# Score products over all 128 rows, and weights laid out tile by tile, in a hybrid decoder layer

## The chip, the cores and the metric

The kernel runs on one core of a Trainium2 chip. The metric is device time in microseconds (us) from one launch to its end. The core has a matrix engine (TensorE, PE in the rows; its weight loads are shown apart as PEld), a vector engine (VectorE, DVE), a scalar engine (ScalarE, ACT), a general engine (GpSimd, POOL), a queue that only issues transfers (SyncE, SP), and 16 DMA engines.

## What is computed

One layer of a decoder on 1024 tokens of width 1024, in float32. The parts that the change touches:

```python
z = rms_norm(x) @ w_in                       # sgu u and v, q, k, value
q, k: 4 heads, 2 maps each, 64 wide          # differential attention
s = q @ k.T - slope * distance, causal       # per head and map
a = softmax(s[map 0]) - lam * softmax(s[map 1]);  o = a @ v
x = x + concat(sgu, o) @ w_out
x = x + memory_attention(x, mem)             # w_q_mem, w_kv_mem, w_o_mem; 256 memory tokens
x = x + moe(x)                               # top group, then top 2 of its 8 experts; 32 experts
#   expert: (silu(xb @ w_gate[e]) * (xb @ w_up[e])) @ w_down[e]
```

## The kernel before

A float32 product is built from three products of rounded parts: high by high, low by high, high by low (the helper mm3, L141 to L143). So each weight tile is loaded raw (128 partitions by 1024 numbers, 512 KB), then copied on ACT to a rounded high part whi (L286) and subtracted on DVE to a low part wlo (L287). One list, plan, holds all weight tiles in the order of use. pump issues the loads from SP (L277) a set number of tiles ahead, and take hands a split tile to the stage that uses it. SP is a queue in program order: a load that waits holds up the loads behind it. raw, whi, wlo and the larger activations share one pool of 45 slots of 512 KB (unit), so a load can also wait for a slot to come free.

The source of a tile decides its runs, the stretches of memory that are contiguous for one partition. A tile of 128 columns of w_in, w_kv_mem or w_out is read in runs of 512 B, a pair tile of 256 columns (w_in, md) and the memory tokens (memT) in runs of 1 KB, w_gate and w_up in runs of 2 KB, and w_down, w_q_memT and w_o_mem in runs of 4 KB. md and vwd are products of memory and weights that the kernel itself writes to DRAM (from POOL's queue) and reads back as weight tiles: md is written in runs of 1 KB; vwd is written in runs of 4 KB and read in runs of 512 B.

The program runs in this order: projections of the first head (0 to 35 us; x tiles come in on SP among the first weight tiles), memory keys and values with 16 tiles of w_kv_mem (35 to 92), attention with the other projections as filler between its steps (68 to 410), products of memory and weights and the output projection (403 to 580), memory attention (580 to 800), routing (to 843), the 32 experts (843 to 1430), and a final norm. A planner (Merge) fixes the order within a stage by estimated costs; the engines then follow that order.

In attention, a head has four tiles for q and k of 128 partitions by 1024 tokens, and one for k's low part. qa holds map 0's rounded q in partitions 0 to 63 and its low part in 64 to 127; qb holds map 1's the other way round. ka and kb hold the rounded k, once in each half of the partitions; the second half is a copy by a DMA on POOL's queue (L579, 64 by 512 numbers, 128 KB; four per head, for ka and kb and for each half of the tokens). kl holds k's low part, map 0 in partitions 0 to 63 and map 1 in 64 to 127. The score of a block of 128 queries is then, for each map and each piece of up to 512 keys, one product over 128 rows, q (high and low) by k's high part (L632), and one over 64 rows, q's high part by k's low part (L633). Their sum goes to DVE (L635), then ACT (L639) and POOL (L646).

The gate and up products of an expert use 8 tiles, the down product 4. From expert 16 on the loads run at most 10 tiles ahead (before that, up to 31).

Of the kernel before, what the change touches and what calls it, by code (L numbers as in the profile page):

```python
# [8 lines left out]
F32 = mybir.dt.float32  # L9
F32R = mybir.dt.float32r  # L10
# [8 lines left out]
S = 1024  # L19
D = 1024  # L20
# [94 lines left out]
def tile_layer(tc, a, out):  # L115
# [71 lines left out]

    kmd = dram.tile([128, KT, 256], F32, name="kmd")
    vmd = dram.tile([128, KT, 256], F32, name="vmd")
    md = dram.tile([D, D], F32, name="md")  # L190
    vwd = dram.tile([D, D], F32, name="vwd")
    mixd = dram.tile([896, S], F32, name="mixd")
    x1d = dram.tile([D, S], F32, name="x1d")
    x2d = dram.tile([S, D], F32, name="x2d")
# [18 lines left out]

    plan = []

    def add_cols(w, c0):
        plan.append((w[:, c0:c0 + 128], 8))

    def add_pair(w, c0):
        for q in range(2):  # L220
            plan.append((w[q * 512:(q + 1) * 512, c0:c0 + 256], 4))

    w_in = a["w_in"]
    for item in (SEQ1 + " " + SEQ2).split():
        kind, i = item[0], int(item[1:])
        if kind == "s":
            add_pair(w_in, 512 + 256 * i)
            add_cols(w_in, 256 * i)
            add_cols(w_in, 256 * i + 128)
        elif kind == "k":  # L230
            for c in range(4 * i, 4 * i + 4):
                add_cols(a["w_kv_mem"], c * 128)
        elif kind in "qx":
            add_cols(w_in, 1024 + 128 * i)
            add_cols(w_in, 1536 + 128 * i)
        elif kind == "v":
            add_pair(w_in, 2048 + 256 * i)
        elif kind == "f":
            add_cols(a["w_out"], i * 128)
        else:  # L240
            w = a["w_q_memT" if kind == "m" else "w_o_mem"]
            for k in (2 * i, 2 * i + 1):
                plan.append((w[k * 128:(k + 1) * 128, :], 1))
    for hd in range(4):
        add_pair(md, hd * 256)
    for h in range(2):
        for f in range(8):
            add_cols(vwd, f * 128)
    wg, wu, wd = a["w_gate"], a["w_up"], a["w_down"]

    work = [("g", 0)]
# [5 lines left out]
    for kind, e in work:  # L257
        if kind == "g":
            for w in (wg, wu):
                for q in range(4):  # L260
                    plan.append((w[e, q * 256:(q + 1) * 256, :], 2))
        else:
            for k in range(4):
                plan.append((wd[e, k * 128:(k + 1) * 128, :], 1))
# [5 lines left out]
    def pump():  # L270
        while ptr["load"] < min(len(plan), ptr["use"] + ahead["load"]):
            j = ptr["load"]
            src, k = plan[j]
            raw = unit("raw", [128, 1024])
            r3_, s3 = raw.rearrange("p (k c) -> p k c", k=k), src.rearrange("(k p) c -> p k c", p=128)
            for i in ((0, 4), (4, 8)) if j == 0 else ((0, k),):
                nc.sync.dma_start(r3_[:, i[0]:i[1]], s3[:, i[0]:i[1]])  # L277
            raws[j] = raw
            ptr["load"] += 1
        while ptr["split"] < min(ptr["load"], ptr["use"] + ahead["split"]):  # L280
            j = ptr["split"]
            raw = raws.pop(j)
            hi = unit("whi", [128, 1024], F32R)
            lo = unit("wlo", [128, 1024], F32R)
            for c in (slice(0, 512), slice(512, 1024)) if j == 0 else (slice(0, 1024),):
                nc.scalar.copy(hi[:, c], raw[:, c])  # L286
                ahead.get("lo", nc.vector).tensor_tensor(lo[:, c], raw[:, c], hi[:, c].bitcast(F32), op=OP.subtract)  # L287
            parts[j] = (hi, lo)
            ptr["split"] += 1
# [11 lines left out]

    def load_mem(q):
        m = unit("memt", [128, 4, 256])
        nc.sync.dma_start(m, a["memT"][q * 512:(q + 1) * 512, :].rearrange("(k p) t -> p k t", p=128))
        memt.append(m)

    def split_mem(q):
# [83 lines left out]
    def mem_m(hd):  # L391

        kk = kks.pop(("m", hd))
        w = [take() for _ in range(2)]
        for g in range(2):
            mt = unit("mt", [128, 4, 256])
            for b in range(2):
                p = ps1("pp")
                for j in range(2):
                    ds_ = slice((4 * g + 2 * b + j) * 128, (4 * g + 2 * b + j + 1) * 128)  # L400
                    for d in range(2):
                        mm3(p[:, j * 256:(j + 1) * 256], w[d][0][:, 0, ds_], w[d][1][:, 0, ds_], kk[:, 0, d],
                            kk[:, 1, d], d == 0, d == 1)
                nc.scalar.copy(mt[:, 2 * b:2 * b + 2], p)
                yield 1.3, 0.0
            nc.gpsimd.dma_start(md[g * 512:(g + 1) * 512, hd * 256:(hd + 1) * 256].rearrange(
                "(k p) c -> p k c", p=128), mt)

    def mem_w(hd):

        vk = kks.pop(("w", hd))
        w = [take() for _ in range(2)]
        for b in range(2):
            bs_ = slice(b * 128, (b + 1) * 128)
            mt = unit("mt", [128, D])
            for c in range(2):
                cs = slice(c * 512, (c + 1) * 512)
                p = ps1("pp")
                for d in range(2):
                    mm3(p, vk[:, 0, d, bs_], vk[:, 1, d, bs_], w[d][0][:, 0, cs], w[d][1][:, 0, cs], d == 0, d == 1)  # L420
                nc.scalar.activation(mt[:, cs], p, AF.Copy, scale=mcol[:, b:b + 1])
                yield 1.3, 0.0
            nc.gpsimd.dma_start(vwd[hd * 256 + b * 128:hd * 256 + (b + 1) * 128, :], mt)


    hTh = [None] * KT
# [126 lines left out]

    def evacs(hd):

        r0, r1 = slice(0, 64), slice(64, 128)

        def evac_q(h, p):
            hs = slice(h * H, (h + 1) * H)
            if h == 0:  # L560
                qk[hd] += [unit(n, [128, S], F32R) for n in ("qa", "qb")]
            qa, qb = qk[hd]
            q = scaled(h, p)
            sc = 0.125 / slopes[hd]
            for t, r, o in ((qa, r0, r1), (qb, r1, r0)):
                nc.scalar.activation(t[r, hs], q[r], AF.Copy, scale=sc)
                nc.vector.scalar_tensor_tensor(t[o, hs], q[r], sc, t[r, hs].bitcast(F32), op0=OP.mult,
                                               op1=OP.subtract)

        def evac_k(h, p):  # L570
            hs = slice(h * H, (h + 1) * H)
            if h == 0:
                qk[hd] += [unit(n, [128, S], F32R) for n in ("ka", "kb", "kl")]
            ka, kb, kl = qk[hd][2:]
            k = scaled(h, p)
            for t, r, o in ((ka, r0, r1), (kb, r1, r0)):
                nc.scalar.copy(t[r, hs], k[r])
                nc.vector.tensor_sub(kl[r, hs], k[r], t[r, hs].bitcast(F32))
                KQ(nc).dma_start(t[o, hs], t[r, hs])  # L579

        return evac_q, evac_k

# [26 lines left out]
    def scores():  # L609
# [5 lines left out]
        for hd in range(4):  # L615
            for x in until(("qk", hd)):
                yield x
            qa, qb, ka, kb, kl = qk.pop(hd)
            for i in range(8):
                if 8 * hd + i - 2 * ndone[0] >= NA:  # L620
                    yield 0.0, lambda: 8 * hd + i - 2 * ndone[0] < NA
# [2 lines left out]
                stt = sm.tile([128, 8], F32, name="stt", bufs=4)  # L624
                pr = []
                for m in range(2):
                    r = slice(m * 64, m * 64 + 64)
                    q, k = (qa, ka) if m == 0 else (qb, kb)
                    s = ps2("ps_s")
                    for c0 in range(0, nk, 512):  # L630
                        c1 = min(nk, c0 + 512)
                        mm(s[:, c0:c1], q[:, q0:q0 + 128], k[:, c0:c1], start=True, stop=False)  # L632
                        mm(s[:, c0:c1], q[r, q0:q0 + 128], kl[r, c0:c1], start=False, stop=True)  # L633
                    pe = half("p%d" % m) if i < HP else unit("p%d" % m, [128, S])
                    nc.vector.tensor_tensor_reduce(out=pe[:, :nk], in0=s[:, :nk], in1=bias[:, 896 - q0:1024],  # L635
                                                   scale=1.0, scalar=NEG, op0=OP.add, op1=OP.max,
# [837 lines left out]
    with tc.If(nr > 0):  # L1474
# [59 lines left out]
        with tc.For_i(0, nr, 1) as b:  # L1534
# [16 lines left out]
            for w in (wg, wu):  # L1551
                p = ps1()
                for q in range(4):
                    raw = unit("oraw", [128, 2, 512])
                    nc.sync.dma_start(raw, w[bass.ds(eb, 1), q * 256:(q + 1) * 256, :].rearrange(
                        "a (k p) c -> p (a k) c", p=128))
                    for k2 in range(2):
                        k = 2 * q + k2
                        mm(p, xt[:, k * 128:(k + 1) * 128], raw[:, k2], start=(k == 0), stop=(k == KT - 1))
# [62 lines left out]
def _arrays(inp):  # L1622
# [2 lines left out]
    f = {n: np.asarray(v) for n, v in inp.items()}  # L1625
    r = {}
    r["xT"] = c(f["x"][0].T)
    r["memT"] = c(f["mem"][0].T)
    for n in ("norm_mix", "norm_xq", "norm_mem", "norm_ffn"):
        r[n] = c(f[n][0].reshape(8, 128).T)  # L1630
    r["norm_ffn_row"] = c(f["norm_ffn"])
# [6 lines left out]
    for n in ("lambda_q1", "lambda_k1", "lambda_q2", "lambda_k2", "b_router_group", "b_router_expert"):  # L1638
        r[n] = c(f[n])
    r["w_q_memT"] = c(f["w_q_mem"][0].T)  # L1640
    for n in ("w_in", "w_out", "w_kv_mem", "w_o_mem", "w_router_group", "w_router_expert", "w_gate",
              "w_up", "w_down"):
        r[n] = c(f[n][0])
    return {"in_" + n: v for n, v in r.items()}


# [18 lines left out]
```

## Time and profile before

| | before |
|---|---|
| median of 3 runs | 1466.63 us (1462.87 to 1467.89) |
| the profiled execution | 1463.22 us, its span 1461.5 us |
| busy in the span: PE, DVE, ACT, POOL | 1365.2, 1008.1, 834.6, 255.4 us |
| packets moved by DMA | 188088, 320.28 MB; 86179 of them under 2 KB |

The profile follows one execution. Busy time counts an engine's own instructions; a matrix product's start is exact, while its end is modelled, so the pace of products is read from one start to the next. "Idle before" of an instruction is the time its engine waited, with what released it. PEclk is the granted clock of TensorE as a share of full speed.

### The profile page before, as it was taken

What the parts mean: (1) busy time and instruction counts of PE and PEld (TensorE: products, weight loads), DVE (VectorE), ACT (ScalarE), POOL (GpSimd) and SP (SyncE); (2) the same over time, 40 slices, a digit from 0 to 9 for tenths busy, and PEclk for the clock granted to TensorE, in tenths of its full rate; (3) what the DMA queues carried; (4) which work ended last, traced back from release to release, by engine and by line L of the source; (5) the groups of instructions that cost most, each with busy time, mean ns of one, the idle gap of its engine ahead of it and who ended that gap; (6) DMA issues with size and microseconds to landing.
All of it is one profiled execution on the core that took longest, in us unless ns stands there. A gap on an engine that the chain in (4) does not pass through costs nothing. (4 is left out here: it accounts for less than half of the span.)

```text
span 1461.5 us, 20484 instructions
## 1 busy us (share of the span) xinstructions
PE 1365.2 (93%) x7420; PEld 1153.7 (79%) x7420; DVE 1008.1 (69%) x1593; ACT 834.6 (57%) x1136; POOL 255.4 (17%) x273
## 2 busy tenths in 40 slices
PE   7989999999999999999999589999989999999981
PEld 5887878878878888999888468888778888877860
DVE  6745666656667544333454779999979999988875
ACT  7533444334445544332322368888868888777863
POOL 3131110211002222112112211111111111111012
PEclk9989999999999999999999699999999999999995
DMA  9540101102046676113699599999999899999984
GB/s 295 160 112 1 44 30 59 58 29 66 30 150 205 225 239 206 35 37 99 179 306 348 193 314 322 361 330 350 344 365 347 303 366 345 354 359 359 362 283 196
DMA packets 188088, 320.28 MB, mean 219 GB/s; under 512 B 15491, under 2 KB 86179, under 8 KB 187984
## 3 DMA queue, kind: packets, MB, share of 16 engines
q1 hardware_dynamic: 163040, 272.14, 53.5%
q0 software_dynamic: 16496, 38.41, 9.1%
q10 hardware_dynamic: 8448, 8.39, 1.7%
q8 instruction: 59, 0.97, 0.3%
q14 instruction: 45, 0.37, 0.1%
HBM read 287.10 MB, written 46.66 MB: 228 GB/s over the span
## 5 line engine op out<-in xcount | busy, mean ns | idle before, releaser
L287 DVE TENSOR_TENSOR wlo<-raw,whi 128x1024 fp32r<-128x1024 f32 (+1 forms) x467 | 554.7, 1226 | 99.2 <-ACT whi L286 82.6
L286 ACT CAST whi<-raw 128x1024 fp32r<-128x1024 f32 (+1 forms) x469 | 473.9, 1049 | 85.0 <-DMA raw<-in_w_down 21.9
L141 PE MATMUL pgu<-whi,xth 128*128 128x512 f32 x512 | 199.2, 398 | 7.6 <-ACT whi L286 7.6
L142 PE MATMUL pgu<-wlo,xth 128*128 128x512 f32 x512 | 201.7, 394 | 1.4 <-DVE wlo L287 1.4
L143 PE MATMUL pgu<-whi,xtl 128*128 128x512 f32 x512 | 201.4, 393 | 0.3 <-DVE xtl L147 0.3
L1415 POOL DMA_INDIRECT x2d<-y,idx x31 | 50.9, 1643 | 471.1 <-ACT y L1414 413.4
L141 PEld LDWEIGHTS pgu<-whi,xth 128*128 128x128 f32 x512 | 97.3, 190 | 29.5 <-ACT whi L286 10.0
L142 PEld LDWEIGHTS pgu<-wlo,xth 128*128 128x128 f32 x512 | 97.4, 190 | 23.2 <-DVE wlo L287 2.1
L143 PEld LDWEIGHTS pgu<-whi,xtl 128*128 128x128 f32 x512 | 97.1, 190 | 20.5 <-DVE xtl L147 0.7
L142 PE MATMUL py<-wlo,ht 128*128 128x512 f32 x256 | 104.7, 409 | 5.1 <-DVE wlo L287 5.0
L141 PE MATMUL py<-whi,ht 128*128 128x512 f32 x256 | 103.5, 404 | 4.2 <-ACT whi L286 2.5
L143 PE MATMUL py<-whi,ht 128*128 128x512 f32 x256 | 101.5, 396 | 0.0
L639 ACT ACTIVATE p<-p,stt 128x128 f32<-128x128 f32 (+7 forms) x64 | 49.6, 775 | 69.0 <-DVE stt L638 62.3
L635 DVE CUSTOM_DVE_ANT_0 p<-ps_s,bias 128x128 f32<-128x128 f32 (+7 forms) x64 | 47.8, 754 | 41.6 <-PE ps_s L633 39.7
L141 PE MATMUL pp<-whi,hTh 128*128 128x256 f32 x256 | 75.7, 296 | 0.0
L142 PE MATMUL pp<-wlo,hTh 128*128 128x256 f32 x256 | 74.6, 291 | 0.7 <-DVE wlo L287 0.7
L143 PE MATMUL pp<-whi,hTl 128*128 128x256 f32 x256 | 74.6, 292 | 0.0
L141 PE MATMUL pp<-whi,h2h 128*128 128x256 f32 x256 | 73.1, 285 | 0.0
L142 PE MATMUL pp<-wlo,h2h 128*128 128x256 f32 x256 | 72.5, 283 | 0.0
L143 PE MATMUL pp<-whi,h2l 128*128 128x256 f32 x256 | 72.5, 283 | 0.0
L141 PE MATMUL pp<-hTh,whi 128*128 128x512 f32 x160 | 64.0, 400 | 0.0
L142 PE MATMUL pp<-hTl,whi 128*128 128x512 f32 x160 | 62.9, 393 | 0.0
(359 smaller groups left out, 2986.4 us busy)
## 6 DMA issues: line engine op xcount, KB each, us to landing
raw<-in_w_gate SPq DMA_DIRECT2D x128, 512.0 KB
raw<-in_w_up SPq DMA_DIRECT2D x128, 512.0 KB
raw<-in_w_down SPq DMA_DIRECT2D x128, 512.0 KB
raw<-in_w_in SPq DMA_DIRECT2D x19, 512.0 KB
raw<-in_w_kv_mem SPq DMA_DIRECT2D x16, 512.0 KB
raw<-vwd SPq DMA_DIRECT2D x16, 512.0 KB
raw<-in_w_q_memT SPq DMA_DIRECT2D x8, 512.0 KB
raw<-in_w_out SPq DMA_DIRECT2D x8, 512.0 KB
```

The costliest lines, as they stand in the source:

```text
L141: mm(o, sh, mh, start=start, stop=False)
L142: mm(o, sh, ml, start=False, stop=False)
L143: mm(o, sl, mh, start=False, stop=stop)
L286: nc.scalar.copy(hi[:, c], raw[:, c])
L287: ahead.get("lo", nc.vector).tensor_tensor(lo[:, c], raw[:, c], hi[:, c].bitcast(F32), op=OP.subtract)
L635: nc.vector.tensor_tensor_reduce(out=pe[:, :nk], in0=s[:, :nk], in1=bias[:, 896 - q0:1024], scale=1.0, scalar=NEG, op0=OP.add, op1=OP.max, ...
L639: nc.scalar.activation(pe[:, :nk], pe[:, :nk], AF.Exp, bias=stt[:, 2 + m:3 + m], scale=slopes[hd], accum_out=stt[:, 4 + m:5 + m])
L1415: nc.gpsimd.indirect_dma_start(out=x2d[:, :], out_offset=bass.IndirectOffsetOnAxis(ap=idx[:, e:e + 1], axis=0), in_=y, in_offset=None, bou ...
```

## The change

The score's second product takes all 128 rows. k's low part now has two tiles, la and lb, each with its numbers in both halves of the partitions, as ka and kb have them; the second halves are copied by four more DMAs per head on POOL's queue. The product thus also adds low part by low part. The weights are laid out on the host so that each tile is one contiguous piece and each partition's 1024 numbers are one run of 4 KB (w_in in the two forms w_in8 and w_in4, w_kv_mem, w_out, memT, w_gate, w_up). md is written and read in runs of 4 KB; vwd is read in runs of 4 KB and written in runs of 512 B.

```diff
-    md = dram.tile([D, D], F32, name="md")
-    vwd = dram.tile([D, D], F32, name="vwd")
+    md = dram.tile([8, 128, 1024], F32, name="md")
+    vwd = dram.tile([8, 128, 1024], F32, name="vwd")
...
-    def add_cols(w, c0):
-        plan.append((w[:, c0:c0 + 128], 8))
+    def add_cols(w, i):
+        plan.append((w[i], 8))
-    def add_pair(w, c0):
+    def add_pair(w, i):
         for q in range(2):
-            plan.append((w[q * 512:(q + 1) * 512, c0:c0 + 256], 4))
+            plan.append((w[2 * i + q], 4))
...
-                    plan.append((w[e, q * 256:(q + 1) * 256, :], 2))
+                    plan.append((w[e, q], 2))
...
-            r3_, s3 = raw.rearrange("p (k c) -> p k c", k=k), src.rearrange("(k p) c -> p k c", p=128)
-            for i in ((0, 4), (4, 8)) if j == 0 else ((0, k),):
-                nc.sync.dma_start(r3_[:, i[0]:i[1]], s3[:, i[0]:i[1]])
+            for i in ((0, 512), (512, 1024)) if j == 0 else ((0, 1024),):
+                nc.sync.dma_start(raw[:, i[0]:i[1]], src[:, i[0]:i[1]])
...
-            nc.gpsimd.dma_start(md[g * 512:(g + 1) * 512, hd * 256:(hd + 1) * 256].rearrange(
-                "(k p) c -> p k c", p=128), mt)
+            nc.gpsimd.dma_start(md[2 * hd + g], mt.rearrange("p k c -> p (k c)"))
...
-            nc.gpsimd.dma_start(vwd[hd * 256 + b * 128:hd * 256 + (b + 1) * 128, :], mt)
+            ks = slice((2 * hd + b) * 128, (2 * hd + b + 1) * 128)
+            nc.gpsimd.dma_start(vwd[:, :, ks].rearrange("f p c -> p f c"), mt.rearrange("p (f c) -> p f c", f=KT))
...
-                qk[hd] += [unit(n, [128, S], F32R) for n in ("ka", "kb", "kl")]
+                qk[hd] += [unit(n, [128, S], F32R) for n in ("ka", "kb", "la", "lb")]
...
-            for t, r, o in ((ka, r0, r1), (kb, r1, r0)):
+            for t, l, r, o in ((ka, la, r0, r1), (kb, lb, r1, r0)):
                 nc.scalar.copy(t[r, hs], k[r])
-                nc.vector.tensor_sub(kl[r, hs], k[r], t[r, hs].bitcast(F32))
                 KQ(nc).dma_start(t[o, hs], t[r, hs])
+                nc.vector.tensor_sub(l[r, hs], k[r], t[r, hs].bitcast(F32))
+                KQ(nc).dma_start(l[o, hs], l[r, hs])
...
-                        mm(s[:, c0:c1], q[r, q0:q0 + 128], kl[r, c0:c1], start=False, stop=True)
+                        mm(s[:, c0:c1], q[:, q0:q0 + 128], kl[:, c0:c1], start=False, stop=True)
```

SP issues the same loads in the same order as before. On POOL's queue, the first head's copies stand between the writes of the memory keys (kmd). Before:

```order
L331 DMA kmd<-km 128x256 x5
L579 DMA ka<-ka 64x512
L579 DMA kb<-kb 64x512
L579 DMA ka<-ka 64x512
L579 DMA kb<-kb 64x512
L331 DMA kmd<-km 128x256 x3
```

The same place in the changed kernel (its lines are numbered one lower here):

```order
L330 DMA kmd<-km 128x256 x5
L578 DMA ka<-ka 64x512
L580 DMA la<-la 64x512
L578 DMA kb<-kb 64x512
L580 DMA lb<-lb 64x512
L578 DMA ka<-ka 64x512
L580 DMA la<-la 64x512
L578 DMA kb<-kb 64x512
L580 DMA lb<-lb 64x512
L330 DMA kmd<-km 128x256 x3
```

Four copies have become eight, each copy of a low part behind that of the high part. On PE, the first block of scores stands between products of memory keys (pmk). Before:

```order
L143 MATMUL pmk<-mh,wlo 128x256
L632 MATMUL ps_s<-ka,qa 128x128
L633 MATMUL ps_s<-kl,qa 128x128
L632 MATMUL ps_s<-kb,qb 128x128
L633 MATMUL ps_s<-kl,qb 128x128
L141 MATMUL pmk<-mh,whi 128x256
L142 MATMUL pmk<-ml,whi 128x256
```

The same place in the changed kernel:

```order
L143 MATMUL pmk<-mh,wlo 128x256
L632 MATMUL ps_s<-ka,qa 128x128
L633 MATMUL ps_s<-la,qa 128x128
L632 MATMUL ps_s<-kb,qb 128x128
L141 MATMUL pmk<-mh,whi 128x256
L142 MATMUL pmk<-ml,whi 128x256
L633 MATMUL ps_s<-lb,qb 128x128
```

The last low product has moved behind two products of memory keys; the number of score products is the same.

## Rows read from the trace of the kernel before

**Rows 1.** Windows: us, busy (instructions) of PE, PEld, DVE, ACT, POOL; PEclk, DMA share, GB/s.

```profile
100.00:403.00 303.00, 301.20 (x1759) 248.02 (x1758) 188.02 (x541) 131.41 (x260) 41.12 (x64) 0.99 0.14 39
403.00:580.00 177.00, 171.42 (x890) 146.26 (x890) 98.77 (x158) 88.17 (x128) 39.34 (x41) 0.99 0.62 206
843.00:1430.00 587.00, 566.60 (x2616) 462.97 (x2616) 514.57 (x479) 467.46 (x506) 90.75 (x62) 0.99 0.97 343
```

**Rows 2.** Timeline of PE around a block of scores: start, us, instruction.

```profile
148.73 0.39 PE L141 MATMUL pp<-hTh,whi 128*128 128x512 f32 x1
148.96 0.39 PE L142 MATMUL pp<-hTl,whi 128*128 128x512 f32 x1
...
149.56 0.49 PE L674 MATMUL pt<-ident,p 128*128 128x128 f32 x3
149.81 0.48 PE L632 MATMUL ps_s<-ka,qa 128*128 128x512 f32 x1
150.22 0.50 PE L633 MATMUL ps_s<-kl,qa 64*128 64x512 f32 x1
150.64 0.49 PE L632 MATMUL ps_s<-ka,qa 128*128 128x512 f32 x1
```

**Rows 3.** Timeline of the weight loads at the same place.

```profile
148.73 0.19 PEld L142 LDWEIGHTS pp<-hTl,whi 128*128 128x128 f32 x1
...
150.21 0.18 PEld L633 LDWEIGHTS ps_s<-kl,qa 64*128 64x128 f32 x1 [0.24 <-issue]
```

**Rows 4.** One line's instructions: L633 on PE for map 0, with its widths.

```profile
L633 PE MATMUL ps_s<-kl,qa x48: 322/492/793, 67.9 to 400.9; 64*128 64x512 f32 x24, 64*128 64x128 f32 x8, 64*128 64x256 f32 x8, 64*128 64x384 f32 x8
```

**Rows 5.** Timeline of PE: score products alone and of the smaller widths.

```profile
125.12 0.39 PE L632 MATMUL ps_s<-ka,qa 128*128 128x512 f32 x1
125.44 0.49 PE L633 MATMUL ps_s<-kl,qa 64*128 64x512 f32 x1
125.86 0.33 PE L632 MATMUL ps_s<-ka,qa 128*128 128x128 f32 x1
126.12 0.32 PE L633 MATMUL ps_s<-kl,qa 64*128 64x128 f32 x1
...
140.39 0.44 PE L632 MATMUL ps_s<-ka,qa 128*128 128x384 f32 x1
140.76 0.43 PE L633 MATMUL ps_s<-kl,qa 64*128 64x384 f32 x1
```

**Rows 6.** Waits of SP's queue: us in total, times, longest.

```profile
SPq L277 <- DVE at L147: 133.2, 5, 68.2
```

**Rows 7.** Timeline at the first scores, POOL's copies and PE.

```profile
67.33 0.51 POOL L579 DMA_DIRECT2D kb<-kb  x1
67.64 0.30 PE L632 MATMUL ps_s<-ka,qa 128*128 128x128 f32 x1 [2.31 <-DMA ka<-ka]
```

**Rows 8.** DMA view, 0 to 50 us: GB/s in 40 slices of 1.25 us.

```profile
GB/s 0 10 222 284 298 304 315 301 380 406 413 410 410 403 406 365 351 328 296 290 292 290 289 290 290 270 232 248 153 273 17 1 184 329 35 220 285 85 20 34
```

**Rows 9.** Timeline of ACT in the first stage.

```profile
9.57 1.05 ACT L286 CAST whi<-raw 128x1024 fp32r<-128x1024 f32 x1 [1.20 <-DMA raw<-in_w_in]
11.30 1.05 ACT L286 CAST whi<-raw 128x1024 fp32r<-128x1024 f32 x1 [0.68 <-DMA raw<-in_w_kv_mem]
12.59 1.15 ACT L150 ACTIVATE hTh<-xt,c_mix 128x1024 fp32r<-128x1024 f32 x1 [0.23 <-DMA xt<-in_xT]
```

**Rows 10.** Windows of one expert's period and of six, columns as in Rows 1.

```profile
1226.46:1244.15 17.69, 17.69 (x86) 14.73 (x84) 16.38 (x16) 14.56 (x17) 3.01 (x2) 1.00 0.97 342
1279.52:1393.56 114.04, 109.60 (x506) 87.88 (x505) 98.02 (x90) 90.09 (x97) 14.49 (x9) 1.00 1.01 361
```

**Rows 11.** Waits of ACT, 1290 to 1400 us: us in total, times, longest.

```profile
ACT whi L286 <- DMA raw<-in_w_down: 19.8, 13, 2.5
```

**Rows 12.** DMA view, 1290 to 1400 us: GB/s in 40 slices of 2.75 us.

```profile
GB/s 341 328 299 375 378 385 382 329 332 311 314 400 400 387 297 364 358 350 378 392 400 361 302 310 339 369 407 405 309 349 399 375 378 407 344 328 387 383 393 376
```

More of the change, by code (lines that the diff above doesn't have):

```diff
@@ L214, in tile_layer @@
     plan = []
-    def add_cols(w, c0):
-        plan.append((w[:, c0:c0 + 128], 8))
-    def add_pair(w, c0):
+    def add_cols(w, i):
+        plan.append((w[i], 8))
+    def add_pair(w, i):
         for q in range(2):
-            plan.append((w[q * 512:(q + 1) * 512, c0:c0 + 256], 4))
-    w_in = a["w_in"]
+            plan.append((w[2 * i + q], 4))
+    w_in8, w_in4 = a["w_in8"], a["w_in4"]
     for item in (SEQ1 + " " + SEQ2).split():
@@ L226, in tile_layer @@
         if kind == "s":
-            add_pair(w_in, 512 + 256 * i)
-            add_cols(w_in, 256 * i)
-            add_cols(w_in, 256 * i + 128)
+            add_pair(w_in4, i)
+            add_cols(w_in8, 2 * i)
+            add_cols(w_in8, 2 * i + 1)
         elif kind == "k":
             for c in range(4 * i, 4 * i + 4):
-                add_cols(a["w_kv_mem"], c * 128)
+                add_cols(a["w_kv_mem"], c)
         elif kind in "qx":
-            add_cols(w_in, 1024 + 128 * i)
-            add_cols(w_in, 1536 + 128 * i)
+            add_cols(w_in8, 4 + i)
+            add_cols(w_in8, 8 + i)
         elif kind == "v":
-            add_pair(w_in, 2048 + 256 * i)
+            add_pair(w_in4, 2 + i)
         elif kind == "f":
-            add_cols(a["w_out"], i * 128)
+            add_cols(a["w_out"], i)
         else:
@@ L244, in tile_layer @@
     for hd in range(4):
-        add_pair(md, hd * 256)
+        add_pair(md, hd)
     for h in range(2):
         for f in range(8):
-            add_cols(vwd, f * 128)
+            add_cols(vwd, f)
     wg, wu, wd = a["w_gate"], a["w_up"], a["w_down"]
@@ L303, in load_mem @@
         m = unit("memt", [128, 4, 256])
-        nc.sync.dma_start(m, a["memT"][q * 512:(q + 1) * 512, :].rearrange("(k p) t -> p k t", p=128))
+        nc.sync.dma_start(m.rearrange("p k t -> p (k t)"), a["memT"][q])
         memt.append(m)
@@ L572, in evac_k @@
             if h == 0:
-                qk[hd] += [unit(n, [128, S], F32R) for n in ("ka", "kb", "kl")]
-            ka, kb, kl = qk[hd][2:]
+                qk[hd] += [unit(n, [128, S], F32R) for n in ("ka", "kb", "la", "lb")]
+            ka, kb, la, lb = qk[hd][2:]
             k = scaled(h, p)
-            for t, r, o in ((ka, r0, r1), (kb, r1, r0)):
+            for t, l, r, o in ((ka, la, r0, r1), (kb, lb, r1, r0)):
                 nc.scalar.copy(t[r, hs], k[r])
-                nc.vector.tensor_sub(kl[r, hs], k[r], t[r, hs].bitcast(F32))
                 KQ(nc).dma_start(t[o, hs], t[r, hs])
+                nc.vector.tensor_sub(l[r, hs], k[r], t[r, hs].bitcast(F32))
+                KQ(nc).dma_start(l[o, hs], l[r, hs])
         return evac_q, evac_k
@@ L617, in scores @@
                 yield x
-            qa, qb, ka, kb, kl = qk.pop(hd)
+            qa, qb, ka, kb, la, lb = qk.pop(hd)
             for i in range(8):
@@ L626, in scores @@
                 for m in range(2):
-                    r = slice(m * 64, m * 64 + 64)
-                    q, k = (qa, ka) if m == 0 else (qb, kb)
+                    q, k, kl = (qa, ka, la) if m == 0 else (qb, kb, lb)
                     s = ps2("ps_s")
@@ L1554, in tile_layer @@
                     raw = unit("oraw", [128, 2, 512])
-                    nc.sync.dma_start(raw, w[bass.ds(eb, 1), q * 256:(q + 1) * 256, :].rearrange(
-                        "a (k p) c -> p (a k) c", p=128))
+                    nc.sync.dma_start(raw.rearrange("p k c -> p (k c)"),
+                                      w[bass.ds(eb, 1), q].rearrange("a p c -> p (a c)"))
                     for k2 in range(2):
@@ L1627, in _arrays, with tiles @@
     r["xT"] = c(f["x"][0].T)
-    r["memT"] = c(f["mem"][0].T)
+    def tiles(w, k, n):
+        q = 8 // k
+        return c(w.reshape(q, k, 128, -1, n).transpose(3, 0, 2, 1, 4).reshape(-1, 128, k * n))
+    r["memT"] = tiles(f["mem"][0].T, 4, 256)
     for n in ("norm_mix", "norm_xq", "norm_mem", "norm_ffn"):
@@ L1640, in _arrays @@
     r["w_q_memT"] = c(f["w_q_mem"][0].T)
-    for n in ("w_in", "w_out", "w_kv_mem", "w_o_mem", "w_router_group", "w_router_expert", "w_gate",
-              "w_up", "w_down"):
+    for n in ("w_o_mem", "w_router_group", "w_router_expert", "w_down"):
         r[n] = c(f[n][0])
+    w = f["w_in"][0]
+    r["w_in8"] = tiles(np.concatenate([w[:, :512], w[:, 1024:2048]], 1), 8, 128)
+    r["w_in4"] = tiles(np.concatenate([w[:, 512:1024], w[:, 2048:]], 1), 4, 256)
+    for n in ("w_out", "w_kv_mem"):
+        r[n] = tiles(f[n][0], 8, 128)
+    for n in ("w_gate", "w_up"):
+        r[n] = c(f[n][0].reshape(32, 4, 2, 128, 512).transpose(0, 1, 3, 2, 4).reshape(32, 4, 128, 1024))
     return {"in_" + n: v for n, v in r.items()}
```

## The prediction

> **What bounds the kernel now.** I read the windows by stage first, then the timeline of PE and its weight loads inside attention, then the waits and the DMA view of the two stages where transfers could be late. In attention PE is busy for 301.20 of 303 us, while DVE has 188.02 and the DMA engines 0.14 of their time [rows 1]: what shortens PE's work there shortens the stage, until something else comes due. In the experts the DMA engines are at 0.97 and PE at 566.60 of 587 us, so PE and the loads are nearly level [rows 1]. The second view shows that PE's time in attention is not all work. Ordinary products of 512 columns start 0.23 us apart, at 148.73 and 148.96 [rows 2]. Inside a block of scores the starts lie 0.41 to 0.42 us apart, at 149.81, 150.22 and 150.64 [rows 2]. The weight load of a score product starts only after an idle 0.24 us put down to issue, where that of the ordinary product at 148.96 starts at 148.73, with the product before it, and waits for nothing [rows 3]. Score products alternate between 128 and 64 rows, and only they do; so I read the gap as the load waiting for the product in flight whenever the rows in use change.
>
> **The score part: what it removes.** There are 192 score products: 48 for each of two maps and two lines, by width 24 of 512, 8 each of 384, 256 and 128 [rows 4]. Per pair (high and low):
> - 512 columns: alone 0.32 + 0.42 = 0.74 us (125.12, 125.44, 125.86 [rows 5]), in a block 0.41 + 0.42 = 0.83 [rows 2]; at the ordinary pace 2 x 0.23 = 0.46. 48 pairs save 0.28 to 0.37 each, 13.4 to 17.8 us.
> - 384 columns: 2 x 0.37 = 0.74 [rows 5] against 0.35 by proportion; 16 pairs, 6.2 us.
> - 128 columns: 2 x 0.26 = 0.52 [rows 5] against 0.17 (three transposes of that width start and end inside 0.25 us, 149.56 to 149.81 [rows 2]); 5.6 us.
> - 256 columns: between, 2 x 0.315 against 0.23; 6.4 us.
>
> The sum is 32 to 36 us; I take 33 as what PE can lose, since the last product of a block already releases an ordinary load. How much of it reaches the end? PE had 1.8 us of idle in the stage, so all of it does as long as PE stays the bound; afterwards PE has some 270 us of work against DVE's 188. But scores go by DVE, ACT and POOL before their values come back to PE, and these chains keep their length while the PE work between them shrinks, and the loads wait for slots: SP waits 133.2 us in five waits, up to 68.2, for slots that DVE frees [rows 6]. I take four fifths, 27 us, with bounds 15 and 33.
>
> A rule of the Trainium skill speaks against this part. What the row shows: a 64-row load takes 0.18 us and a 128-row one 0.19, and it is the idle time ahead of it that makes the pace [rows 3]. "TensorE: Matmul & The Clock Gate", section "LDWEIGHTS (loading the stationary operand)", says that a load's time goes by columns and not by the number of rows. On the load itself the trace agrees (0.18 and 0.19 us); by that rule alone the part would give nothing, and the sum would be about 8 us; the 0.24 us ahead of the load is not in the rule.
>
> **The score part: what it adds.** Sixteen more copies (128 KB) on POOL's queue, 0.51 us of issue each [rows 7], 8 us of POOL, which is busy for 41 of 303 us [rows 1]: hidden, except for the first head. There PE waits 2.31 us for the copy of ka at 67.64 while POOL is still issuing kb at 67.33 [rows 7]. Two more issues now stand ahead of that last kb (0.51 us each), and lb's copy comes last, for which PE waits after two products of memory keys. I take +1 us; the bounds are 0 and +3. One more slot of 45 per head is held while a head lives. I cost it at nothing because the loads of attention use 0.14 of the DMA time; without that cover it is a rival below. The low by low products cost no column more.
>
> **The layout part.** Same bytes, fewer packets.
> - First stage: while runs of 512 B are read, 284 to 315 GB/s; while x comes in runs of 2 KB, 380 to 413; back in 512 B tiles, 290 [rows 8]. Ahead of the x tiles stand 1.5 MB of weights (w_in 1 MB, w_kv_mem 0.5 MB). At 290 GB/s these 1.57 million bytes take 5.4 us, at 405, 3.9. ACT waits for these tiles (1.20 and 0.68 us) and for x behind them until 12.59 [rows 9], and PE runs behind ACT; so -1.5 us, bounds 0 and -2.5. After that PE works on products already loaded.
> - 403 to 580: vwd's eight writes have eight times the runs. At the rates of 290 and 405 GB/s they take 1.8 instead of 1.3 us each, and POOL's issue of them may grow. PE has 171.42 busy of 177 us there, POOL 39.34, DMA 0.62 [rows 1], and vwd is only read a stage later. I cost it at 0; bounds 0 and +2.
> - Experts: a free period is 17.69 us. From 1279.52 to 1393.56 six periods take 114.04 instead of 6 x 17.69 = 106.1, so 7.9 us are lost [rows 10]. In that stretch ACT waits 19.8 us in 13 waits for w_down tiles [rows 11], which stand behind the gate and up tiles in SP's order, and the DMA engines are at 1.01 with 361 GB/s [rows 10]. The slices there go between 300 and 407 GB/s [rows 12]. The gate and up tiles, 4.2 MB of an expert's 6.3, are what changes. At best they go from the mean of 361 to the 405 of the best slices: 11.6 us to 10.4, 1.2 us less per expert. At worst nothing, since runs of 2 KB already gave 410 in the first stage [rows 8]. I take 0.7. A starved period is 19.0 us (114.04 / 6), 1.3 over the free one; 0.7 less leaves 0.6. In the stretch before, at 1226, the period is still free with the DMA engines at 0.97 [rows 10]: PE lives there on the lead of the loads (up to 10 tiles). With less than half of the deficit the lead lasts more than twice as long, which I take to reach past the last of these experts. So nearly all of the 7.9 us comes back: I take -7.5, bounds -3 and -10 (the last expert too).
>
> **Sum.** -27 - 1.5 + 1 - 7.5 = -35 us against the profiled execution, 1463.2: 1428. That one is 3.4 us under the median of the runs (1466.6), from which the sum gives 1431.6. I say 1430.
>
> **The rivals.** Less than 0.3% (4.4 us) either way is about what a measurement of this kernel cannot tell from no change.
> - *Attention stops being bound by PE* (0.15). If the values come back from DVE, ACT and POOL too late for the shorter blocks, PE idles and only about 12 of 33 us come through: 1445. For it: scores' DVE work is the one stage between PE and itself, and the order interleaves them by the longer blocks. Against: DVE's 188 of 303 us leave room [rows 1].
> - *Rows are not the cause* (0.05). The low product keeps its 0.42 us: only the layout's -9 and the +1 remain: 1457.
> - *Bigger runs do not raise the rate* (0.10). "DMA: Bandwidth & Descriptors", section "Specifications", gives 512 B as enough for the full rate and some 358 GB/s as a core's share of the memory. As a mechanism of this kernel: the starved experts stay at 361 GB/s [rows 10], and with it the lost 7.9 us, and the first stage gains nothing: -27 + 1, 1439. Against it speak 290 beside 410 GB/s in the first stage [rows 8] and the slices over 400 among the experts [rows 12].
> - *Slower* (0.05): the extra slot. SP's queue is in order, and its loads wait for slots already [rows 6]. With la and lb two heads alive hold two slots more; if that moves a projection's loads behind the release of a head, PE waits for them with nothing to fill in. It decides if those stalls pass 35 us, e.g. five loads of 8 us each; at 50 us the time would be 1480.
>
> **How the numbers follow.** Forecast as summed, with 22 to 33 us from attention and 4 to 9 from the experts: 0.62, its own range 1420 to 1440. With the rivals at 0.15, 0.10, 0.05 and 0.05, 0.03 stays for no change by a mixture of part gains and stalls. The range must leave out no more than 0.2: it takes in the forecast, the rate rival (1439) and most of the first rival (1445): 1414 to 1448. Faster 0.92, same 0.03, slower 0.05.
>
> **What would show it.** In attention: starts of score products about 0.23 us apart for 512 columns, weight loads without the 0.24 us of idle, PE's busy time near 270 us and idle time of it under 6 us. At the first scores: a wait of some 3 us in all. In the first 20 us: 380 GB/s or more from the start, x's second tile on ACT about 1.5 us before 12.59. Among the experts: the six periods within 107 us, and ACT's waits for w_down nearly gone. The prediction is wrong if PE idles in attention for more than 15 us, if the low product's pace stays at 0.4 us, or if the experts' loads stay at 361 GB/s with the same lost time.

## The result and the profile after

The changed kernel takes 1421.28 us (median of 4 runs, 1418.57 to 1423.17), against 1464.75 of before on the same chip: 43.5 us less, a ratio of 0.9701 (95% interval 0.9673 to 0.9729). The forecast was 1430 with a range of 1414 to 1448. The profiled execution's span went from 1461.5 to 1419.9 us, 41.6 less. The difference of 1.9 us between the two is of the kind that the run with only gate and up tiles explains below.

The stage view of attention after, with columns as in [rows 1] (us; busy and count of PE, PEld, DVE, ACT, POOL; PEclk, DMA share, GB/s), then of the experts:

```profile
102.00:369.00 267.00, 264.25 (x1754) 242.30 (x1753) 184.88 (x538) 127.31 (x254) 47.43 (x76) 0.99 0.19 49
...
812.00:1389.00 577.00, 562.02 (x2616) 462.13 (x2614) 514.10 (x476) 465.51 (x505) 88.47 (x61) 0.99 0.95 348
```

The attention window has the instructions of a like one of before (300.40 us, 1753 products):

```profile
99.60:400.00 300.40, 298.60 (x1753) 247.02 (x1751) 186.18 (x537) 128.70 (x257) 41.52 (x64) 0.98 0.14 38
```

PE still fills it: 2.75 us of idle, where that one had 1.80. POOL has 6 us more, the copies' issues. A block of scores, to be held against [rows 2] and [rows 3]: PE's timeline, then that of its weight loads.

```profile
145.05 0.48 PE L632 MATMUL ps_s<-ka,qa 128*128 128x512 f32 x1
145.37 0.40 PE L633 MATMUL ps_s<-la,qa 128*128 128x512 f32 x1
145.60 0.40 PE L632 MATMUL ps_s<-ka,qa 128*128 128x512 f32 x1
145.84 0.40 PE L633 MATMUL ps_s<-la,qa 128*128 128x512 f32 x1
```

```profile
145.14 0.19 PEld L633 LDWEIGHTS ps_s<-la,qa 128*128 128x128 f32 x1
145.37 0.19 PEld L632 LDWEIGHTS ps_s<-ka,qa 128*128 128x128 f32 x1
```

From the second product of the block on the starts lie 0.23 us apart instead of 0.42 (the first distance, behind the transposes, is 0.32). The load at 145.14 comes before the end of the product before it, without the 0.24 us of idle.

What did not become faster is the first block, to be held against [rows 7]. PE's timeline there:

```profile
65.00 0.30 PE L632 MATMUL ps_s<-ka,qa 128*128 128x128 f32 x1 [0.92 <-DMA ka<-ka]
66.12 0.30 PE L633 MATMUL ps_s<-la,qa 128*128 128x128 f32 x1 [0.83 <-DMA la<-la]
70.24 0.44 PE L632 MATMUL ps_s<-kb,qb 128*128 128x128 f32 x1 [3.82 <-DMA kb<-kb]
```

Three waits, 5.6 us together, stand where one of 2.3 stood. In a second profile of the same kernel (its repeat, below) they are 0.89, 0.87 and 3.10 us, 4.9 together.

The rates of the first 50 us answer to [rows 8], ACT's timeline of the first stage to [rows 9]:

```profile
GB/s 0 28 297 297 298 349 367 403 406 419 419 416 419 406 403 416 410 413 406 403 416 410 180 0 16 259 157 190 229 0 20 269 236 46 272 213 85 20 0 46
```

```profile
8.74 1.05 ACT L285 CAST whi<-raw 128x1024 fp32r<-128x1024 f32 x1 [0.77 <-DMA raw<-in_w_in]
10.03 1.05 ACT L285 CAST whi<-raw 128x1024 fp32r<-128x1024 f32 x1 [0.24 <-DMA raw<-in_w_kv_mem]
11.31 1.15 ACT L150 ACTIVATE hTh<-xt,c_mix 128x1024 fp32r<-128x1024 f32 x1 [0.23 <-DMA xt<-in_xT]
```

From about 9 us on the loads run at 403 to 419 GB/s, w_kv_mem's too, which came at 290 before. x's second tile is taken up by ACT at 11.31 instead of 12.59.

Six experts' periods (the windows view, as in [rows 10]), and ACT's waits in them (us in total, times, longest), as in [rows 11]:

```profile
1246.81:1353.49 106.68, 106.44 (x505) 88.37 (x504) 98.20 (x91) 87.08 (x95) 14.10 (x9) 1.00 0.99 367
```

```profile
ACT whi L285 <- DMA raw<-in_w_down: 7.5, 7, 2.1
```

Of 7.9 us lost there, 0.5 are left (106.68 against 6 x 17.69 = 106.14). ACT still waits for some tiles, but no longer so late that PE does.

Followed along PE's program by the starts of the same products, the span's 41.6 us come about so (hTh is the rounded high part of x times the norm's weights; sgw is a tile that the sgu part loads):

| stretch | forecast, us | measured, us |
|---|---|---|
| first stage, to its last product | -1.5 | -1.3 |
| first block of scores | +1 | +2.8 |
| to the sgw products (97.5 before) | 0 | +0.5 |
| attention, first to last product of hTh as moving data | -27 | -34.6 |
| to the end of the output projection (580 before) | 0 | +2.7 |
| memory attention and routing, to expert 0's transposes | 0 | -1.6 |
| experts | -7.5 | -9.9 |
| after them | 0 | -0.3 |

Four of these rows also hold a difference of the granted clock between the two profiles: attention, the stretch behind it, routing, and the end of the experts. The rows that show it stand with the run with only gate and up tiles.

Where attention's gain sits can be worked out from the starts of all products between the first and the last product of hTh as moving data, each start to the next, stretches of low clock included. The score products took 62.1 us of the 299.3 before and 33.5 of the 264.7 after. The product right behind a block took 13.6 and 8.5, the one right in front of it 6.8 and 6.3, and all others 216.7 and 216.4. So 33.7 of the 34.6 us lie in the score products and in the products right behind them.

### The profile page after: what moved, and what is told of

Its sections match the earlier page's. It is cut to its first block, busy times and chain, and to the rows that moved or that the text cites. A ratio compares the mean times of both kernels' runs of the same rounds, so it can differ in the third digit from the quotient of the medians.

```text
span 1419.9 us, 20537 instructions
## 1 busy us (share of the span) xinstructions
PE 1324.5 (93%) x7420; PEld 1147.9 (81%) x7420; DVE 1006.7 (71%) x1593; ACT 832.9 (59%) x1136; POOL 263.9 (19%) x289
## 4 chain that ended last, share of the span: by engine, by line
PE 69%; DMA 15%; DVE 7%; issue 5%; ACT 3%; POOL 1%; SPq 0%; POOLq 0%; ACTq 0%; DVEq 0%
PE pp L141 11%; PE pp L142 11%; PE pp L143 11%; PE pgu L142 5%; PE pgu L143 5%; PE pgu L141 5%; DMA raw<-in_w_gate 4%; DMA raw<-in_w_down 4%; DMA raw<-in_w_up 3%; PE py L141 3%; PE py L143 3%; PE py L142 3%; PE px L1369 1%; DVE wlo L286 1%; DMA x2d<-y,idx 1%
## 5 line engine op out<-in xcount | busy, mean ns | idle before, releaser
L143 PE MATMUL pp<-hTh,wlo 128*128 128x512 f32 x160 | 63.5, 397 | 0.0
```

The lines of the kernel that those rows point to most:

```text
L143: mm(o, sl, mh, start=False, stop=stop)
```

## The experiments

**The score part alone.** The edits of evacs and scores, with the weights laid out as before.

> The score part alone, the weights laid out as before. If the score part's gain does not depend on the layout, this run gives what attention gave in the changed kernel: 34.6 us less between the first and the last projection of attention, 3 us more at the first scores, so 31 to 33 us less than before (some 1433), and the experts still lose some 8 us to late loads. If faster loads were part of attention's gain (attention gained 34.6 where 33 was the most that the pace of the products gives), it gives only 25 to 28 us.

It took 1430.8 us (1425.43 to 1434.13) against 1466.2, ratio 0.9766 (0.9741 to 0.9791). The same group of products as the lines' view gives it (duration in ns, first and last start), for before, the changed kernel and this one:

```profile
L141 PE MATMUL pp<-whi,hTh x256: 277/283/561, 99.6 to 398.9; 128*128 128x256 f32 x128
```

```profile
L141 PE MATMUL pp<-whi,hTh x256: 274/283/562, 101.7 to 366.4; 128*128 128x256 f32 x128
```

```profile
L141 PE MATMUL pp<-whi,hTh x256: 273/283/563, 102.0 to 366.5; 128*128 128x256 f32 x128
```

From first to last it is 299.3, 264.7 and 264.5 us: attention's gain is the score part's alone, and the layout carries none of it. The time as a whole fell by 35.4 us, some 2 us more than expected. The granted clock is a likely part of it: over the 15 runs of before it goes from 0.960 to 0.967, the lower ones with the longer times, and the median run has 0.962, where the profile that the expectation was worked out from has 0.966. Among the experts the late loads stay:

```profile
1242.73:1356.20 113.47, 108.96 (x506) 87.94 (x504) 97.26 (x90) 89.63 (x96) 14.56 (x9) 1.00 1.00 360
```

```profile
ACT whi L286 <- DMA raw<-in_w_down: 17.6, 12, 2.6
```

These are the windows view of the same six periods, 7.3 us longer than free ones, and ACT's waits in them.

**The layout alone.** The score's lines as before.

> The layout alone, scores as before. If the two parts add up, 9 to 11 us less than before: 1.3 in the first stage, about 8 among the experts, a few tenths to 1 around the routing. If the layout also carries part of attention's gain, 13 to 17 us less. Score products keep starts 0.42 us apart in a block.

1455.48 us (1451.5 to 1460.66) against 1466.2: 10.7 less, ratio 0.9926 (0.9905 to 0.9948). Its six periods:

```profile
1284.03:1391.23 107.20, 106.82 (x505) 88.36 (x504) 97.60 (x90) 86.78 (x95) 14.75 (x9) 1.00 0.99 365
```

So the late loads go with the layout. Score products start 0.41 to 0.43 us apart as before. The two parts, 35.4 and 10.7 us alone, give 46.1 if added; together they gave 43.5 to 45.4. Within the spread of the runs they add up.

**Only w_gate and w_up in runs of 4 KB.** The host lays these two out as in the change; all else is as before.

```diff
-                    plan.append((w[e, q * 256:(q + 1) * 256, :], 2))
+                    plan.append((w[e, q], 0))
...
+            if k == 0:
+                nc.sync.dma_start(raw, src)
```

> Of the layout only w_gate and w_up in runs of 4 KB. If the runs of these tiles are what starved the experts, the six periods before the last expert but one take 106 to 107 us as in the changed kernel, and the time falls by 7 to 9 us; w_in and w_kv_mem then give the 1.3 us that is missing against the whole layout. If packets of 2 KB are already as fast and the gain came from elsewhere, under 2 us.

1460.17 us (1455.64 to 1463.91) against 1466.2: 6.0 less, ratio 0.9964 (0.9947 to 0.998), a little under the 7 to 9 expected. The six periods are free:

```profile
1282.34:1388.59 106.25, 106.25 (x506) 88.40 (x505) 97.91 (x91) 86.86 (x95) 14.17 (x9) 1.00 1.00 367
```

That settles which tiles starved the experts. How it comes about can be worked out from the traces that give each tile's landing: the time that a tile lies ready before ACT splits it, as the median of a dozen tiles in the order of use. With the score part alone (runs of 2 KB) it falls from 12.4 us at the 19th dozen to 0.4 at the 26th, 1.7 per dozen; here it falls from 12.5 to 4.7, 1.1 per dozen, and is used up (0.5) only at the 29th.

The run also shows something about profiles. In attention nothing was changed here, and yet the stretch took 3.0 us longer than in the profile of before. The windows view of two places, this kernel first, then the same work in the kernel before, has the cause in the granted clock (PEclk, the third number from the end):

```profile
199.00:204.00 5.00, 5.00 (x28) 4.79 (x28) 2.73 (x13) 2.22 (x5) 0.00 (x0) 0.66 0.00 0
264.00:269.00 5.00, 5.00 (x22) 4.21 (x22) 4.16 (x14) 1.67 (x2) 0.00 (x0) 0.66 0.01 2
```

```profile
198.00:203.00 5.00, 5.00 (x35) 4.31 (x36) 3.67 (x19) 1.92 (x4) 0.00 (x0) 1.00 0.00 0
263.00:268.00 5.00, 5.00 (x28) 4.29 (x28) 4.16 (x14) 1.66 (x2) 0.00 (x0) 1.00 0.01 2
```

At 0.66 of 5 us, 1.7 us are lost at each place to a stretch at 1.2 GHz; PE was busy all the time in all four windows. So the same work has such stretches in some executions and not in others, and a stage's length in a single profile carries some 3 us of this. The profile of before had one in attention that cost 3.4 us (0.72 over 12 us from 376), the changed kernel's one that cost 1.7 (0.62 over 4.5 us from 250):

```profile
376.00:388.00 12.00, 12.00 (x59) 9.81 (x58) 5.25 (x28) 3.50 (x10) 0.69 (x1) 0.72 0.00 0
```

```profile
250.00:254.50 4.50, 4.50 (x14) 3.56 (x13) 2.71 (x11) 0.21 (x1) 0.00 (x0) 0.62 0.02 5
```

Of attention's 34.6 us, 1.7 are therefore the clock's, and 32.9 the change's. It may not be chance alone: between 110 us and the end of attention the clock takes 3.4, 6.8, 6.8 and 8.5 us in the profiles with the score lines of before (before, layout alone, gate and up alone, copies without use), and 1.7 in all six with 128 rows throughout.

The same holds behind attention. There the changed kernel lost 2.7 us and the layout alone 3.6. The windows view of 39 us each for before, the changed kernel and the layout alone:

```profile
436.00:475.00 39.00, 35.08 (x228) 31.70 (x229) 28.51 (x40) 21.24 (x32) 10.13 (x9) 0.96 0.63 210
```

```profile
402.50:441.50 39.00, 34.02 (x206) 30.14 (x206) 25.79 (x36) 20.32 (x28) 9.12 (x8) 0.91 0.63 210
```

```profile
436.00:475.00 39.00, 34.24 (x200) 30.53 (x201) 25.37 (x35) 20.00 (x28) 8.64 (x8) 0.87 0.62 212
```

By these clocks the changed kernel loses some 2 us more there than before, the layout alone 3.5: about 1 us of the 2.7 is left, and next to nothing of the 3.6. Routing has it the other way round (before, then the changed kernel), and so has the end of the experts:

```profile
796.00:835.00 39.00, 19.19 (x108) 16.85 (x108) 25.92 (x79) 8.98 (x13) 9.31 (x6) 0.56 0.60 212
1420.00:1428.00 8.00, 6.14 (x20) 4.95 (x21) 4.52 (x12) 5.86 (x9) 1.06 (x1) 0.79 1.00 376
```

```profile
765.00:804.00 39.00, 19.24 (x121) 17.03 (x120) 27.13 (x79) 9.32 (x13) 9.82 (x7) 0.61 0.65 225
1379.00:1387.00 8.00, 5.45 (x25) 4.44 (x26) 4.96 (x13) 5.31 (x8) 1.06 (x1) 1.00 0.94 341
```

That is the size of the 1.6 us gained around routing, and 1.7 us of what the experts gained.

**Both score products over 64 rows.** The kernel before, with q's low part by k's high part left out.

```diff
-                        mm(s[:, c0:c1], q[:, q0:q0 + 128], k[:, c0:c1], start=True, stop=False)
+                        mm(s[:, c0:c1], q[r, q0:q0 + 128], k[r, c0:c1], start=True, stop=False)
```

> Kernel before, but the high product too takes only the 64 rows of its map (q's low part by k's high part is left out), so that within a map's products the rows in use do not change. If it is the change between 64 and 128 rows that makes a weight load wait, products of 512 columns within a map start about 0.23 us apart and only the first after a change of rows (into the block, from map 0 to map 1, out of the block) pays 0.2 us: some 60 to 70 percent of the 33 us come back, 18 to 24 us less than before. If a product over 64 rows is slow by itself, all starts lie 0.42 us apart and the time is that of before or a little more.

1449.63 us (1448.64 to 1452.51) against 1466.2: 16.6 less, ratio 0.9891 (0.9866 to 0.9916). A pair of 512 columns alone, on PE and its loads:

```profile
119.72 0.50 PE L632 MATMUL ps_s<-ka,qa 64*128 64x512 f32 x1
119.83 0.19 PEld L633 LDWEIGHTS ps_s<-kl,qa 64*128 64x128 f32 x1
120.06 0.39 PE L633 MATMUL ps_s<-kl,qa 64*128 64x512 f32 x1
...
120.38 0.19 PEld L142 LDWEIGHTS pp<-wlo,hTh 128*128 128x128 f32 x1 [0.37 <-issue]
```

The load of the second 64-row product (119.83) is done while the first runs, and the load of the 128-row product behind the pair (120.38) has the wait. A product over 64 rows is thus not slow by itself; the wait stands at the change of rows. It comes at the borders of a block of scores only, so a part of the 33 us returns. The expectation's size, 18 to 24, was a little too high: most blocks are one or two pairs, and each pays at its borders. Counted from start to start as above, the score products take 41.3 us here (62.1 before, 33.5 with 128 rows), but the product in front of a block takes 12.8 (6.8 and 6.3) and the one behind it 14.8 (13.6 and 8.5). A block with both maps shows something else:

```profile
145.80 0.49 PE L632 MATMUL ps_s<-ka,qa 64*128 64x512 f32 x1
145.82 0.50 PE L632 MATMUL ps_s<-kb,qb 64*128 64x512 f32 x1
146.14 0.39 PE L633 MATMUL ps_s<-kl,qa 64*128 64x512 f32 x1
146.16 0.39 PE L633 MATMUL ps_s<-kl,qb 64*128 64x512 f32 x1
```

Products over rows 0 to 63 and over rows 64 to 127 start 0.02 us apart. They run side by side. So the 16.6 us hold two effects, the wait that is gone and the products side by side.

**Copies and slot without their use.** The changed kernel, with the low product over the 64 rows of its map again (q[r] by la[r] or lb[r]).

> The changed kernel with la, lb and their copies, but the low product over the 64 rows of its map again. It has the copies and the extra slot without their use. If these cost only the first scores' wait, it is 2 to 4 us over the layout alone (1455): 1457 to 1460, with the score products at 0.42 us again. If the slot or the longer queue holds up loads in attention, 1465 or more.

1457.69 us (1456.03 to 1460.78) against 1466.85, ratio 0.9925 (0.9902 to 0.9949); the layout alone had 0.9926. Its median is 2.2 us above that of the layout alone, which is within the spread of the two, so the sixteen copies and the extra slot cost little beyond the waits at the first block (5.4 us in its profile). The slower rival, loads held up by the extra slot, does not occur.

**The copies of low parts last.** On POOL's queue ka, kb, la, lb in each half.

```diff
                 nc.vector.tensor_sub(l[r, hs], k[r], t[r, hs].bitcast(F32))
+            for l, r, o in ((la, r0, r1), (lb, r1, r0)):
                 KQ(nc).dma_start(l[o, hs], l[r, hs])
```

> The changed kernel with both copies of low parts behind both copies of high parts on POOL's queue (ka, kb, la, lb in each half). If the wait of 3.8 us for kb comes from the issues of la ahead of it, the wait for kb falls by some 0.5 us and that for la and lb rises: within 1 us of the changed kernel. If the order alone was the cause, 2 us or more less.

1418.73 us (1413.94 to 1421.77) against 1466.85, ratio 0.9659 (0.9631 to 0.9686). The first block in its timeline (lines numbered one higher):

```profile
64.83 0.30 PE L633 MATMUL ps_s<-ka,qa 128*128 128x128 f32 x1 [0.92 <-DMA ka<-ka]
65.95 0.30 PE L633 MATMUL ps_s<-kb,qb 128*128 128x128 f32 x1 [0.82 <-DMA kb<-kb]
67.49 0.47 PE L634 MATMUL ps_s<-la,qa 128*128 128x128 f32 x1 [1.24 <-DMA la<-la]
69.14 0.48 PE L634 MATMUL ps_s<-lb,qb 128*128 128x128 f32 x1 [0.64 <-DMA lb<-lb]
```

The waits fall from 5.6 us (4.9 in the changed kernel's second profile) to 3.6, more than the 0.5 us of one issue. So the order on the queue did matter, by more than its issue time: in both orders the third and fourth copy land late. But the place in the row is not what decides. In the changed kernel the next four copies, issued from 65.43 on, all take 5.5 to 6.0 us to land, the first of them too; and before, of the four for the first head, the first two took 3.6 and 3.4 us and the last two 2.2 and 2.5. What the slow ones have in common is a weight load that SP issued just before or while POOL was issuing them. SP's timeline before and after:

```profile
62.49 0.37 SPq L277 DMA_DIRECT2D raw<-in_w_kv_mem  x1
```

```profile
63.99 0.33 SPq L276 DMA_DIRECT2D raw<-in_w_kv_mem  x1
```

The issue of every slow copy ended within 4 us behind the start of such a load; the quick copies at 62.62 and 63.34 of the changed kernel were issued ahead of its load, the quick ones of before 4 us and more behind. No run moved the load, so this is not shown to be the cause.

**Zeros in place of the copies.** The low product keeps its 128 rows, but the other half of la and lb is zero; low by low is left out, as before the change.

```diff
+            if h == 0:
+                nc.gpsimd.memset(la[r1].bitcast(F32), 0.0)
+                nc.gpsimd.memset(lb[r0].bitcast(F32), 0.0)
...
-                KQ(nc).dma_start(l[o, hs], l[r, hs])
```

> The changed kernel without the sixteen copies of low parts: the other half of la and lb is set to zero once per head by GpSimd instead, so the low product still takes 128 rows (it leaves out only low by low). If the copies on POOL's queue are what costs at the first scores (waits of 0.9, 0.8 and 3.8 us there against 2.3 before, and a later start of the sgw weights), that stretch falls back by 2.5 to 3.5 us: 1417 to 1419. If the copies cost nothing and the waits are those for ka and kb alone, it stays at 1421; if the memsets wait for slots on POOL's queue ahead of the copies of ka, it is slower.

1418.93 us (1417.45 to 1419.66) against 1466.85, ratio 0.9663 (0.9644 to 0.9682). Two waits of 1.0 and 0.4 us are left in the first block, right behind it PE waits another 1.0 and 0.5 us for a split weight tile, and the memsets stand in idle time of POOL, ten us ahead (timeline of PE and of POOL):

```profile
65.20 0.30 PE L634 MATMUL ps_s<-ka,qa 128*128 128x128 f32 x1 [1.00 <-DMA ka<-ka]
...
66.05 0.30 PE L634 MATMUL ps_s<-kb,qb 128*128 128x128 f32 x1 [0.41 <-DVE la L582]
...
67.48 0.58 PE L141 MATMUL pmk<-mh,whi 128*128 128x256 f32 x1 [1.01 <-ACT whi L285]
...
68.74 0.58 PE L143 MATMUL pmk<-mh,wlo 128*128 128x256 f32 x1 [0.47 <-DVE wlo L286]
```

```profile
53.54 0.95 POOL L576 MEMSET la<- 64x1024 f32 x1
54.54 0.95 POOL L577 MEMSET lb<- 64x1024 f32 x1
```

Since this is the version that seemed to beat both kernels, it was run again beside the changed one on the same chip.

> The changed kernel once more, beside the version with zeros on the same chip. If the zeros are worth the 2.6 us that the first scores show, this one is 2 to 4 us above it: 1420 to 1423. If the difference of the medians (1421.3 and 1418.9, of different calls) is only the spread of the runs, the two are within 1 us.

> The version with zeros in place of the copies of low parts, beside the changed kernel. If the zeros are worth the 2.6 us that the first scores show: 1417 to 1420, 2 to 4 us under the changed kernel. Otherwise within 1 us of it.

The changed kernel took 1421.08 us (1417.47 to 1422.41; ratio 0.9685, 0.9658 to 0.9711), the zeros 1419.01 (1415.81 to 1420.77; ratio 0.9676, 0.965 to 0.9701). The medians differ by 2.1 us, but the runs overlap, and the profiles do not bear the difference out. By the starts of the same products the version with zeros leads by 1.3 us at the first product of attention and by only 0.1 at the end of the output projection (1.7 and 0.6 for its first profile). So it is not shown that zeros are faster than copies.

## Why the prediction was right

**The score part's gain: right in mechanism, too small in size.** The gap was read as a load that waits whenever the rows in use change. With 128 rows throughout, starts lie 0.23 us apart and the gap is gone; with 64 rows throughout a pair, it is gone inside the pair and stays at its borders. Both say the same, and the rival "rows are not the cause" falls. The mis-sized step is "I take four fifths, 27 us": the whole of the 33 us came through (32.9 after the clock's 1.7). The 33 itself is made up a little differently than summed: 28.6 us came from the score products, and 5.1 from the product right behind a block, which the sum did not have ("the last product of a block already releases an ordinary load"). I had feared that scores would come back too late from DVE, ACT and POOL. PE's idle time in the stage grew from 1.8 to 2.75 us, so those chains had room to spare, and the rival in which attention stops being bound by PE falls too. SP's long waits for slots [rows 6] were no sign of trouble: the longest is still 66.4 us after, and PE waits for split weights in the stage for 1.7 us in all.

On the rule of the Trainium skill that a load's time does not depend on the number of rows, in "TensorE: Matmul & The Clock Gate", section "LDWEIGHTS (loading the stationary operand)": the trace agrees on the load itself (0.18 and 0.19 us). It was no ground against the change, since the cost lay in when the load may start.

**What the score part adds: mis-sized.** "I take +1 us" for the first block; it was +2.8, within the bounds of 0 to 3, and another 0.5 at sgw, whose transfers stand behind the copies on POOL's queue and which I had counted as hidden. In the second profile of the changed kernel the first block is +1.2: its waits are 0.7 us shorter, and the clock, which falls in the waits of the first block in both profiles, comes back sooner (0.71 over 70 to 77 us, where the first profile has 0.53). Two issues of 0.51 us explain only a third of the 2.8. The step also misread [rows 7]: the kb at 67.33 is the copy for the second half of the tokens; the one that the first block needs was issued at 64.52. The copy of kb, issued at 63.87, was there at 70.24, and in the order with the low parts last it was there 2.9 us after its issue (63.09 to 65.95). Why the third and fourth copy in a row land late is open; the runs show that their order on the queue changes it, and that the slow copies are those issued about with or shortly behind a load of w_kv_mem.

**The first stage: right.** -1.3 against -1.5 (-0.8 to -1.4 in the other runs with this layout). The rates came as said only from 9 us on; up to 6 us they stayed near 297 GB/s, though runs were longer there already.

**The experts: right in mechanism, a little too small.** Gate and up tiles in longer runs raised the mean rate only from 361 to 367 GB/s, but that is enough for the lead of the loads to last: 7.4 of 7.9 us came back (gate and up alone: 7.8). That it was enough holds some luck. The sum took "less than half of the deficit"; the lead shrinks by 1.1 to 1.3 us per dozen tiles (one expert's) instead of 1.7, about a third less, and is used up three experts later, in the last of the six periods. The other 2.5 us of the stage lie at its two ends: 1.3 in its first experts, whose cause was not tried, and the rest behind the six periods, where the clock's 1.7 stand.

The Trainium skill's figures in "DMA: Bandwidth & Descriptors", section "Specifications", are 512 B as enough for the full rate and some 358 GB/s as a core's share when two cores share the memory. The first does not hold here: w_kv_mem's tiles came at 290 GB/s in runs of 512 B, and at 403 to 419 as contiguous pieces in runs of 4 KB (both were changed together). The second is no cap for this kernel, which runs on one core and passes it.

**The stretch after attention.** I costed vwd's writes with more runs at 0. That holds: the layout alone lost 3.6 us up to the end of the output projection, and the clock accounts for some 3.5 of them. Of the 2.7 us that the changed kernel lost there the clock accounts for some 2. About 1 us is left, which the score part alone has too (2.6 us, with the clock low at the same two places) and which the gate and up tiles alone have not (0.1); what it is stays open. The 1.6 us gained around routing, forecast as 0, are the clock's.

**The total.** The clock differs in four stretches of these two profiles, by some 3 us together in favour of the changed kernel. Of the 6.6 us by which the two profiles differ more than forecast, some 3 are thus the clock, which the sum had no term for. The rest is attention's 33 in place of 27, less what the first block and the stretch behind attention added.

## What to carry to other kernels

When matrix products of a stream use now 128 rows and now 64, look at the idle time before the weight loads: here each change of rows cost some 0.2 us, as much as a product of 512 columns, and filling the unused rows with a copy or with zeros made the products free of it. Zeros need no transfer, though no gain over the copies is shown. And where a stream of loads is short by a few per cent, a slightly higher rate can take away the whole loss, since what counts is whether the lead lasts to the end; that is worked out from the free and the starved period and from how long tiles lie ready, not from the mean rate.

## What the runs showed of the hardware

- Two products over different halves of the rows start 0.02 us apart and run side by side: eight of 512 columns take from 145.80 to 146.94, 1.14 us, where eight over 128 rows take 1.94 (145.05 to 146.99 in the changed kernel).
- Copies of 128 KB within the core's memory, issued in a row on POOL's queue, land 2.2 to 2.7 us after their issue with no weight load of 512 KB issued in the 4 us before, and 3.4 to 6.4 us after it where one was issued then or at the same time (before, the changed kernel, and the low parts last). That the load is the cause was not tried.
- Stretches at 1.2 GHz appear in PE's busiest stage in some executions of the same work and not in others, at 1.7 or 3.4 us each.
